# Split weights in whole 2048-column slots, low products last, and a third K-tile pair by sums in each FFN input group

## The chip, the cores and the metric

One core of a Trainium2 chip runs the whole program. The metric is the device time of one execution in microseconds (us); times of a kernel are given as the median of its runs, and the profile is one execution taken by the hardware profiler.

## The reference

256 rows of 2048 features go through one layer of four residual blocks, each followed by a layer norm (`alpha` is 2 to the 1/4):

```
def swiglu_ffn(x, w_in, w_out):
    g, u = jnp.split(x @ w_in, 2, axis=-1)
    return (jax.nn.silu(g) * u) @ w_out
...
h = layer_norm(ALPHA * h + 0.5 * swiglu_ffn(h, ffn1_w_in, ffn1_w_out), ...)
h = layer_norm(ALPHA * h + hybrid_mixer(h, w_in, ...), ...)
h = layer_norm(ALPHA * h + memory_cross_attention(h, mem, ...), ...)
h = layer_norm(ALPHA * h + 0.5 * swiglu_ffn(h, ffn2_w_in, ffn2_w_out), ...)
```

`w_in` of an FFN is 2048 x 11008 (a gate half and an up half of 5504 columns), `w_out` 5504 x 2048. The mixer is two attentions (A: 16 heads of 64 with a bias by distance; B: 16 heads with low-rank queries and keys) whose results are gated and projected; the cross attention has four heads of 512 over 256 memory rows. Everything is float32, and nearly all of the work is products with weight matrices that are read once from HBM.

## The kernel before, in words

**Number format.** A float32 operand is kept as two `float32r` tensors: hi is the rounded value, lo is the remainder. A product of weights W and activations X is made of three matmuls into one PSUM bank: W_hi X_hi, W_lo X_hi and W_hi X_lo. Activations are split when they are made (`Act` holds hi and lo of a K-tile of 128 features side by side). Weights are split as they stream through.

**Streaming.** A weight load is 1 MB, 128 partitions by 2048 columns, into one of three `raw` buffers by SP's queue (line 175). `load` (line 192) splits it in pieces of 1024 columns: ScalarE copies the piece to hi (line 212), VectorE subtracts to make lo (line 215). The pieces lie in four hi slots and four lo slots (`UNITS`, the pools `whi` and `wlo`). `run` walks a list of items, each a function with its weights, and emits loads ahead of use as far as the slots reach. The Tile framework then orders each engine's instructions by their priority and adds semaphores, so the order of an engine comes from the place of an item in the list, from `prio` and from the scheduler.

**FFN input groups.** The 5504 hidden columns are cut into ten groups of 512 and one of 384, and worked in two halves (24 and 19 K-tiles): a half's input groups first, then its output products. An input group has 16 K-tiles, loaded as eight pairs (1 MB: gate and up columns of two K-tiles), and four PSUM banks `ps[tt, g]` (two row halves by up and gate). `mm_pair` issues 24 matmuls of 512 columns per pair, the three products of each bank together (line 296). In ten of the eleven groups of each FFN, the pairs named by `SUMS_IN` go through a scheme with seven block products instead of eight (Strassen's, in Winograd's form): `form_sums` makes a tile of sums of the pair's weights on VectorE (line 183), `mm_sums` (line 340) issues 7 x 3 = 21 matmuls, with forms of the activations made once per FFN (`sum_forms`, lines 307 and 311). Four of the seven results go to the other four PSUM banks, `qs[0]` to `qs[3]`, which all pairs by sums of the group share; after the last one `shared` (lines 602 to 607) turns them into four corrections. `product` (lines 648 to 651) adds these to the four banks and computes silu(gate) x up; `turn` (line 663) transposes the result by TensorE during the next group. Two groups in a row use the two sets of four banks in turn. The weights of a pair by sums and its sums take two slots and the blocks X2 and X3.

**FFN output groups** use the same `pair_group` with their own pairs by sums (`SUMS_OUT`); their forms are made by `forms_step` while the last input groups of the half run.

**Wide products.** Most of the mixer and cross projections use `mm_wide`: stationary W, 16 K-tiles of one 1 MB block, each with a matmul of 512 columns (W_hi by X hi and lo side by side, line 264) and one of 256 columns (W_lo by X_hi, line 265), in turn. The blocks are w_lat 9, w_qk 16, w_gate 32, w_o_b 16, w_xk 16 and w_xq 16 of 16 K-tiles, and w_o_a 16 of eight. `mm_feat` (256 columns, line 253) and `mm_tok` (512 columns, line 284) serve the other products.

**Layer norms** sit between the blocks: VectorE adds the last output columns to the residual, gathers statistics (BN_STATS, BN_AGGR, lines 364 and 369), takes the reciprocal root (lines 348 to 353), scales (line 383, with ScalarE's line 385), and TensorE transposes the rows (line 391) for the next block. Leftover products of the block before fill TensorE during that chain.

## Time and profile before

| | |
|---|---|
| median of 3 runs | 2551.24 us (2547.13 to 2551.26) |
| the profiled execution | 2550.92 us |
| its span, first to last instruction | 2549.2 us |
| mean granted TensorE clock | 0.998 |
| HBM read | 482.69 MB, 190 GB/s over the span |
| DMA queue of the weights, share of 16 engines | 50.5% |

The program is one long stream of weight blocks. A busy share on the page is of the whole span; to see what hides what, one looks at a stretch (a table by windows) or at the rows of an engine in time order (a timeline). A row of the timeline gives the start, the duration, engine, line, operation, output and inputs, how many instructions it stands for, and in brackets how long the engine was idle before it and what released it. The durations of matmuls overlap, since TensorE is a pipeline; what a matmul costs is read from one start to the next. The same holds, less strongly, for queued operations of VectorE.

### The profile page before, as it was taken

What the parts mean: (1) busy time and instruction counts of PE and PEld (TensorE: products, weight loads), DVE (VectorE), ACT (ScalarE), POOL (GpSimd) and SP (SyncE); (2) the same over time, 40 slices, a digit from 0 to 9 for tenths busy, and PEclk for the clock granted to TensorE, in tenths of its full rate; (3) what the DMA queues carried; (4) which work ended last, traced back from release to release, by engine and by line L of the source; (5) the groups of instructions that cost most, each with busy time, mean ns of one, the idle gap of its engine ahead of it and who ended that gap; (6) DMA issues with size and microseconds to landing.
All of it is one profiled execution on the core that took longest, in us unless ns stands there. A gap on an engine that the chain in (4) does not pass through costs nothing.

```text
span 2549.2 us, 32108 instructions
## 1 busy us (share of the span) xinstructions
PE 2533.5 (99%) x12608; PEld 2134.7 (84%) x12608; DVE 1844.1 (72%) x2501; ACT 1279.0 (50%) x1732; POOL 30.0 (1%) x87
## 2 busy tenths in 40 slices
PE   9999999999999999999999999999999999999998
PEld 7888888888888888888888888888888888888886
DVE  6787767788776766555557785555788877787886
ACT  5555445555444555544444564454555554455542
POOL 0000000000000000000000000000000000000000
PEclk9999999999999999999999999999999999999999
DMA  6645554545755643345556565544554555455563
GB/s 252 242 179 207 201 197 172 216 163 217 255 171 177 194 138 116 141 175 189 193 188 256 183 216 196 195 155 146 204 193 181 205 208 198 182 198 198 198 234 130
DMA packets 74184, 488.04 MB, mean 191 GB/s; under 512 B 8625, under 2 KB 8881, under 8 KB 20785
## 3 DMA queue, kind: packets, MB, share of 16 engines
q1 hardware_dynamic: 68496, 467.13, 50.5%
q0 software_dynamic: 3808, 15.73, 2.0%
q10 hardware_dynamic: 1728, 3.15, 0.3%
q8 instruction: 98, 1.61, 0.3%
q14 instruction: 54, 0.43, 0.0%
HBM read 482.69 MB, written 2.10 MB: 190 GB/s over the span
## 4 chain that ended last, share of the span: by engine, by line
PE 97%; DVE 1%; DMA 1%; ACT 0%; issue 0%; ACTq 0%; DVEq 0%; SPq 0%
PE at L296 20%; PE mm L284 19%; PE mm L296 17%; PE mm L264 17%; PE mm L265 8%; PE mm L340 5%; PE at L340 5%; PE mm L253 2%; PE at L865 1%; PE at L748 1%; PE at L895 1%; DMA raw<-ffn_w_in_r 1%; DMA H<-xT 0%; PE at L1165 0%; PE at L1143 0%; PE at L391 0%
## 5 line engine op out<-in xcount | busy, mean ns | idle before, releaser
L215 DVE TENSOR_TENSOR lo<-raw,hi 128x1024 fp32r<-128x1024 f32 (+1 forms) x744 | 896.9, 1213 | 558.7 <-ACT hi L212 548.3
L212 ACT CAST hi<-raw 128x1024 fp32r<-128x1024 f32 (+1 forms) x744 | 773.0, 1044 | 864.2 <-PE at L296 188.4
L264 PE MATMUL mm<-T,hi 128*128 128x512 f32 x1168 | 415.1, 399 | 0.0
L296 PE MATMUL mm<-hi,T 128*128 128x512 f32 (+1 forms) x1088 | 330.1, 380 | 1.0 <-ACT hi L243 1.0
L265 PE MATMUL mm<-T,lo 128*128 128x256 f32 x1168 | 328.2, 281 | 0.0
L296 PE MATMUL at<-hi,T 128*128 128x512 f32 x960 | 300.6, 389 | 0.0
L264 PEld LDWEIGHTS mm<-T,hi 128*128 128x128 f32 x1168 | 219.4, 188 | 55.2 <-issue 1.5
L296 PEld LDWEIGHTS mm<-hi,T 128*128 128x128 f32 x1088 | 202.8, 188 | 36.1 <-ACT hi L243 1.5
L264 PE MATMUL mm<-H,hi 128*128 128x512 f32 x640 | 225.9, 397 | 0.0
L265 PEld LDWEIGHTS mm<-T,lo 128*128 128x128 f32 x1168 | 220.7, 189 | 0.1
L296 PEld LDWEIGHTS at<-hi,T 128*128 128x128 f32 x960 | 180.2, 188 | 37.2
L296 PE MATMUL mm<-lo,T 128*128 128x512 f32 (+1 forms) x544 | 207.5, 381 | 0.4 <-DVE lo L244 0.4
L296 PE MATMUL at<-lo,T 128*128 128x512 f32 x480 | 187.6, 391 | 0.0
L265 PE MATMUL mm<-H,lo 128*128 128x256 f32 x640 | 178.9, 280 | 0.0
L284 PE MATMUL mm<-hi,H 128*128 128x512 f32 x568 | 176.3, 389 | 0.0
L296 PE MATMUL at<-hi,H 128*128 128x512 f32 x560 | 174.8, 389 | 0.0
L264 PEld LDWEIGHTS mm<-H,hi 128*128 128x128 f32 x640 | 120.2, 188 | 29.1
L243 ACT CAST X<-raw 128x1024 fp32r<-128x1024 f32 (+1 forms) x104 | 107.3, 1033 | 71.3 <-DVE raw L183 70.7
L243 ACT CAST hi<-raw 128x1024 fp32r<-128x1024 f32 (+2 forms) x122 | 102.0, 843 | 63.5 <-PE mm L296 29.2
L284 PE MATMUL mm<-hi,X 128*128 128x512 f32 x416 | 130.3, 391 | 0.0
L284 PEld LDWEIGHTS mm<-hi,H 128*128 128x128 f32 x568 | 106.6, 188 | 22.0
L244 DVE TENSOR_TENSOR X<-raw,X 128x1024 fp32r<-128x1024 f32 (+1 forms) x104 | 124.5, 1199 | 0.0
(246 smaller groups left out, 3808.1 us busy)
## 6 DMA issues: line engine op xcount, KB each, us to landing
raw<-ffn_w_in SPq DMA_DIRECT2D x150, 1024.0 KB, 4.6
raw<-ffn_w_out SPq DMA_DIRECT2D x66, 1024.0 KB, 5.2
raw<-w_gate SPq DMA_DIRECT2D x32, 1024.0 KB, 4.8
raw<-ffn_w_out_r SPq DMA_DIRECT2D x16, 1024.0 KB, 4.8
raw<-w_qk SPq DMA_DIRECT2D x16, 1024.0 KB, 4.8
raw<-w_o_b SPq DMA_DIRECT2D x16, 1024.0 KB, 4.7
raw<-w_out SPq DMA_DIRECT2D x16, 1024.0 KB, 4.8
raw<-w_xk SPq DMA_DIRECT2D x16, 1024.0 KB, 4.8
```

The costliest lines, as they stand in the source:

```text
L212: self.nc.scalar.copy(hi[:, :m], raw[:, c:c + m])
L215: self.nc.vector.tensor_tensor(lo[:, :m], raw[:, c:c + m], hi[:, :m].bitcast(F32), ALU.subtract)
L243: self.nc.scalar.copy(hi, src)
L244: self.nc.vector.tensor_tensor(lo, src, hi.bitcast(F32), ALU.subtract)
L253: self.nc.tensor.matmul(ps, w[u][wi][:, c:c + P], x.at(xi, kt), start=(j == 0 and k == 0), stop=(j == n - 1 and k == 2),)
L264: self.nc.tensor.matmul(ps, hi, x.both(kt), start=(kt == 0), stop=False)
L265: self.last_mm = self.nc.tensor.matmul(ps[:, :S], lo, x.at(0, kt), start=False, stop=(kt == n - 1))
L284: self.last_mm = self.nc.tensor.matmul(ps, x.at(xi, kt)[:, tt * P:(tt + 1) * P], w[u][wi][:, c:c + 512], start=(start and j == 0 and k == ...
L296: self.last_mm = self.nc.tensor.matmul(ps[tt, g][:, :n], x.at(xi, kt)[:, tt * P:(tt + 1) * P], hi_lo[wi][:, g * n:(g + 1) * n], start=(kt ...
L340: self.last_mm = self.nc.tensor.matmul(bank[:, :m], a[xi], hi_lo[wi][:, c:c + m], start=own and first and j == 0, stop=own and last and j ...
L748: self.nc.tensor.transpose(ps[:, i * P:(i + 1) * P], s[:, c:c + P], self.ident)
L865: nc.tensor.matmul(ps[:, c0:c0 + nk], q[:, tt * P:(tt + 1) * P], k[:, :nk], start=(j == 0), stop=(j == len(parts) - 1))
```

## The change

1. `UNITS` is 2 and a slot holds 2048 columns. `halves` splits a whole load: ScalarE still copies pieces of 1024, and VectorE makes the lo of the whole load in one subtract (line 236 of the changed kernel: 2048 columns; 1536 for the three raw quarters of a pair by sums, which were pieces of 1024 and 512). Over the program VectorE's subtracts and adds of 1024 columns go from 958 to 106, with 409 new ones of 2048 and 86 of 1536; ScalarE's copies of 1024 go from 902 to 942.
2. In every product all matmuls with W_hi of a block come first and those with W_lo last (`mm_feat`, `mm_wide`, `mm_tok`, `mm_pair`, `mm_sums`).
3. `SUMS_IN` is (2, 4, 6) instead of (2, 5). The forms of the third pair lie in four small work tiles, since the block X0 holds two. The three adds of the weights are one of 1024 and two of 512 as before, formed one load ahead; the sums are split into X2 (hi) and X3 (lo) of 2048 columns. Of the program's matmuls, 12424 become 12364.
4. `held` counts slots of the new size. The weights `w_nope` of attention B come two heads to a 1 MB load, which stays in its slot for the odd head; SP's loads go from 476 to 467.

The same in the code:

```diff
-SUMS_IN = (2, 5)
+SUMS_IN = (2, 4, 6)
...
-UNITS = 4
+UNITS = 2
...
         def slots(w):
-            if isinstance(w, Sums):
-                return 2
-            return 0 if w[1] else -(-w[0].shape[1] // 1024)
+            return 0 if isinstance(w, tuple) and w[1] else 1
...
         def form_sums(i):
-            raw, t, m = fetch(i), self.raw_tile(), queue[i].m
-            for a, b, c in ((slice(0, 2 * m), raw[:, 0:2 * m], raw[:, m:3 * m]),
-                            (slice(2 * m, 3 * m), t[:, 0:m], raw[:, 2 * m:3 * m]),
-                            (slice(3 * m, 4 * m), t[:, 2 * m:3 * m], raw[:, 3 * m:4 * m])):
-                self.nc.vector.tensor_tensor(t[:, a], b, c, ALU.add)
-            sums[i] = []
-            for k in range(2):
-                blk = self.block(SUM_TAGS[k], (P, 2, 1024), F32R)
-                self.split(t[:, k * 2 * m:(k + 1) * 2 * m], blk[:, 0, :2 * m], blk[:, 1, :2 * m])
-                sums[i].append((blk[:, 0, :], blk[:, 1, :]))
+            if i < len(queue) and isinstance(queue[i], Sums) and i not in sums:
+                raw, t, m = fetch(i), self.raw_tile(), queue[i].m
+                two = [v.rearrange("p (a m) -> p a m", a=2) for v in (t[:, :2 * m], raw[:, m:3 * m])]
+                self.nc.vector.tensor_tensor(two[0], two[1], raw[:, :m].unsqueeze(1).to_broadcast([P, 2, m]), ALU.add)
+                for a, b in ((2, 0), (3, 2)):
+                    self.nc.vector.tensor_tensor(t[:, a * m:a * m + m], t[:, b * m:b * m + m],
+                                                 raw[:, a * m:a * m + m], ALU.add)
+                sums[i] = t
         def load(i):
             w = queue[i]
             raw = fetch(i)
-            for k in (i, i + 1):
-                if k < len(queue) and isinstance(queue[k], Sums) and k not in sums:
-                    form_sums(k)
-            got = []
+            form_sums(i)
             if isinstance(w, Sums):
-                for a, b in ((2 * w.m, 4 * w.m), (0, w.m)):
-                    hi, lo = self.unit()
-                    self.split(raw[:, a:b], hi[:, :b - a], lo[:, :b - a])
-                    got.append((hi, lo))
-                return got + sums[i]
-            ap, tags = w
-            n = ap.shape[1]
-            if tags:
-                blk = [self.block(g, (P, 2048), F32R) for g in tags[:2]]
-            step = 768 if ap.tensor.name.endswith("_w_in_r") else 1024
-            for c in range(0, n, step):
-                m = min(step, n - c)
-                hi, lo = [x[:, c:c + step] for x in blk] if tags else self.unit()
-                self.nc.scalar.copy(hi[:, :m], raw[:, c:c + m])
-                with self.tc.issue_after(self.chain.ins) if self.chain is not None else nullcontext():
-                    self.nc.vector.tensor_tensor(lo[:, :m], raw[:, c:c + m], hi[:, :m].bitcast(F32), ALU.subtract)
-                got.append((hi, lo))
+                n = 4 * w.m
+                got = self.halves(raw[:, w.m:n], *self.unit()), self.halves(
+                    sums[i][:, :n], *(self.block(g, (P, 2048), F32R) for g in SUM_TAGS))
+            else:
+                ap, tags = w
+                hi, lo = (self.block(g, (P, 2048), F32R) for g in tags[:2]) if tags else self.unit()
+                got = self.halves(raw[:, :ap.shape[1]], hi, lo)
+            form_sums(i + 1)
...
-            units = [u for _ in ws for u in ready.pop(0)]
+            got = [ready.pop(0) for _ in ws]
             live -= sum(slots(queue[done + i]) for i in range(len(ws)))
             done = need
...
+    def halves(self, src, hi, lo):
+        n = src.shape[1]
+        for c in range(0, n, 1024):
+            d = min(c + 1024, n)
+            self.nc.scalar.copy(hi[:, c:d], src[:, c:d])
+        with self.tc.issue_after(self.chain.ins) if self.chain is not None else nullcontext():
+            self.nc.vector.tensor_tensor(lo[:, :n], src, hi[:, :n].bitcast(F32), ALU.subtract)
+        return hi, lo
...
     def mm_wide(self, ps, w, x, n=KT):
+        hi, lo = ([v[:, kt * P:(kt + 1) * P] for kt in range(n)] for v in w)
         for kt in range(n):
-            c = kt % 8 * P
-            hi, lo = (u[:, c:c + P] for u in w[kt // 8])
-            self.nc.tensor.matmul(ps, hi, x.both(kt), start=(kt == 0), stop=False)
-            self.last_mm = self.nc.tensor.matmul(ps[:, :S], lo, x.at(0, kt), start=False, stop=(kt == n - 1))
+            self.nc.tensor.matmul(ps, hi[kt], x.both(kt), start=(kt == 0), stop=False)
+        for kt in range(n):
+            self.last_mm = self.nc.tensor.matmul(ps[:, :S], lo[kt], x.at(0, kt), start=False, stop=(kt == n - 1))
...
     def mm_pair(self, ps, w, n, x, kts, nk=KT):
-        for (hi_lo, kt) in zip(w, kts):
-            for tt in range(2):
-                for g in range(2):
-                    for k, (wi, xi) in enumerate(((0, 0), (1, 0), (0, 1))):
-                        self.last_mm = self.nc.tensor.matmul(
-                            ps[tt, g][:, :n], x.at(xi, kt)[:, tt * P:(tt + 1) * P],
-                            hi_lo[wi][:, g * n:(g + 1) * n],
-                            start=(kt == 0 and k == 0), stop=(kt == nk - 1 and k == 2),
-                        )
+        for wi in range(2):
+            for j, kt in enumerate(kts):
+                for tt in range(2):
+                    for g in range(2):
+                        c = (2 * j + g) * n
+                        for xi in range(2 - wi):
+                            self.last_mm = self.nc.tensor.matmul(
+                                ps[tt, g][:, :n], x.at(xi, kt)[:, tt * P:(tt + 1) * P], w[wi][:, c:c + n],
+                                start=(kt + wi + xi == 0), stop=(kt == nk - 1 and wi == 1),
+                            )
...
-        self.split(f, out[:, 0], out[:, 1])
+        if isinstance(out, list):
+            for j in range(4):
+                self.split(f[:, j], out[j][:, 0], out[j][:, 1])
+        else:
+            self.split(f, out[:, 0], out[:, 1])
...
-                e["f"] = self.block(tag, (P, len(at), 2, 4, P), F32R)
-            self.sum_forms(x(), 2 * at[i], e["f"][:, i])
+                e["block"] = self.block(tag, (P, 2, 2, 4, P), F32R)
+            out = e["block"][:, i] if i < 2 else [self.w1((P, 2, P), F32R) for _ in range(4)]
+            self.sum_forms(x(), 2 * at[i], out)
+            e[i] = [[out[:, a, j, :] if i < 2 else out[j][:, a] for a in (0, 1)] for j in range(4)]
...
-        n5, s2, n3, s3 = ([forms[:, a, j, :] for a in (0, 1)] for j in range(4))
-        for bank, a, (hi_lo, c), own in (
-                (ps[0, 0], plain(k + 1, 0), (u1, m), False),
-                (ps[0, 1], n3, (u1, 0), False),
-                (qs[0], plain(k, 0), (u2, 0), True),
-                (qs[1], n5, (t13, 0), True),
-                (qs[3], s3, (t13, m), True),
-                (qs[2], s2, (t24, 0), True),
-                (ps[1, 0], plain(k + 1, 1), (t24, m), False)):
-            for j, (wi, xi) in enumerate(((0, 0), (1, 0), (0, 1))):
-                self.last_mm = self.nc.tensor.matmul(
-                    bank[:, :m], a[xi], hi_lo[wi][:, c:c + m],
-                    start=own and first and j == 0, stop=own and last and j == 2)
+        n5, s2, n3, s3 = forms
+        for v, parts in (
+                (w[0], ((ps[0, 0], plain(k + 1, 0), 2, False),
+                        (ps[0, 1], n3, 1, False),
+                        (qs[0], plain(k, 0), 0, True))),
+                (w[1], ((qs[1], n5, 0, True),
+                        (qs[3], s3, 1, True),
+                        (qs[2], s2, 2, True),
+                        (ps[1, 0], plain(k + 1, 1), 3, False)))):
+            for wi in range(2):
+                for bank, a, c, own in parts:
+                    for xi in range(2 - wi):
+                        self.last_mm = self.nc.tensor.matmul(
+                            bank[:, :m], a[xi], v[wi][:, c * m:(c + 1) * m],
+                            start=own and first and wi + xi == 0, stop=own and last and wi == 1)
...
-        held = [2 * sum(g is None for g in tags[:j]) for j in range(5)]
+        held = [sum(g is None for g in tags[:j]) for j in range(5)]
...
-            def fn(w):
+            def fn(w=None):
+                if h % 2 == 0:
+                    kept[h + 1] = w
+                else:
+                    w = kept.pop(h)
                 for k in range(2):
                     ps = self.mm_tile()
-                    self.mm_feat(ps[:, :S], w, [(0, k * 512 + j * P) for j in range(4)], self.c,
-                                 range(4 * k, 4 * k + 4))
+                    c = h % 2 * 1024 + k * 512
+                    self.mm_feat(ps[:, :S], w, [c + j * P for j in range(4)], self.c, range(4 * k, 4 * k + 4))
                     v = self.w1()
                     (nc.scalar.copy if k == 0 else nc.vector.tensor_copy)(v, ps[:, :S])
                     bq[h, k] = v
-            self.add(fn, t["w_nope"][h])
-        def b_scores(h):
+            self.add(fn, *(() if h % 2 else (t["w_nope"][h // 2],)), held=h % 2)
+        def b_scores(h, held):
...```

The order of instructions shows it at three places. First VectorE at the end of an input group of the first FFN (`w` are the work tiles of `shared`, `mm` the banks of `qs`, X the low half of the sums, `lo` the low half of a load). Before:

```order
L244 TENSOR_TENSOR lo_1314<-raw_1265,hi_1313 128x512
L215 TENSOR_TENSOR lo_1344<-raw_1341,hi_1343 128x1024
L215 TENSOR_TENSOR lo_1348<-raw_1341,hi_1347 128x1024
L215 TENSOR_TENSOR lo_1375<-raw_1372,hi_1374 128x1024
L604 TENSOR_TENSOR w_244_1384<-w_242_1382,mm_1240 128x512
L215 TENSOR_TENSOR lo_1379<-raw_1372,hi_1378 128x1024
L605 TENSOR_TENSOR w_243_1383<-w_243_1383,w_244_1384 128x512
```

And in the changed kernel:

```order
L236 TENSOR_TENSOR X_189_1293<-raw_1262,X_188_1292 128x2048
L236 TENSOR_TENSOR lo_1324<-raw_1321,hi_1323 128x2048
L603 TENSOR_TENSOR w_198_1358<-w_196_1356,mm_1196 128x512
L236 TENSOR_TENSOR lo_1352<-raw_1349,hi_1351 128x2048
L604 TENSOR_TENSOR w_197_1357<-w_197_1357,w_198_1358 128x512
L605 TENSOR_TENSOR w_198_1358<-w_198_1358,mm_1197 128x512
```

The combinations (604 to 607 before, 603 to 606 now) followed the low half of pair 6 and a part of pair 7's; now they follow pair 7's, and a subtract of 2048 columns, the low half of the next group's first pair, stands inside them where one of 1024 stood.

Second, VectorE where an output group's forms are made during an input group (`L307` and `L311` before, `L300` and `L304` now; X is the low half of the sums of weights, or of the forms where it is 512 wide). Before:

```order
L244 TENSOR_TENSOR X_190_1121<-raw_1117,X_190_1121 128x1024
L651 SCALAR_TENSOR_TENSOR w_181_1048<-w_180_1047,w_181_1048 128x512
L244 TENSOR_TENSOR X_191_1124<-raw_1117,X_191_1124 128x1024
L215 TENSOR_TENSOR lo_1128<-raw_1113,hi_1127 128x1024
L215 TENSOR_TENSOR lo_1132<-raw_1113,hi_1131 128x1024
L311 TENSOR_TENSOR w_198_1137<-w_197_1136 128x128 x2
L311 TENSOR_TENSOR w_198_1137<-w_198_1137,w_197_1136 128x128
```

And in the changed kernel:

```order
L182 TENSOR_TENSOR raw_1082<-raw_1082,raw_1080 128x512
L304 TENSOR_TENSOR w_156_1088<-w_155_1087 128x128
L182 TENSOR_TENSOR raw_1082<-raw_1082,raw_1080 128x512
L304 TENSOR_TENSOR w_156_1088<-w_156_1088,w_155_1087 128x128
L304 TENSOR_TENSOR w_156_1088<-w_155_1087 128x128
L304 TENSOR_TENSOR w_156_1088<-w_155_1087,w_156_1088 128x128
L236 TENSOR_TENSOR lo_1133<-raw_1080,hi_1132 128x1536
L226 TENSOR_TENSOR X_154_1086<-w_156_1088,X_154_1086 128x512
L236 TENSOR_TENSOR X_164_1138<-raw_1082,X_163_1137 128x2048
```

The forms came after the low halves of the sums and now come before them.

Third, TensorE at the start of the mixer, where `mm_wide` begins (`T` are the normed activations, `hi` and `lo` the block's halves). Before:

```order
L264 MATMUL mm_5846<-T_971_5397,hi_5769 128x512
L265 MATMUL mm_5846<-T_971_5397,lo_5770 128x256
L264 MATMUL mm_5846<-T_971_5397,hi_5769 128x512
L265 MATMUL mm_5846<-T_971_5397,lo_5770 128x256
L264 MATMUL mm_5846<-T_971_5397,hi_5769 128x512
```

And in the changed kernel:

```order
L256 MATMUL mm_5496<-T_749_5066,hi_5425 128x512 x4
L256 MATMUL mm_5496<-T_750_5067,hi_5425 128x512 x4
L256 MATMUL mm_5496<-T_751_5068,hi_5425 128x512 x4
L256 MATMUL mm_5496<-T_752_5069,hi_5425 128x512 x4
L258 MATMUL mm_5496<-T_749_5066,lo_5426 128x256 x4
```

The two widths took turns and now stand in two series, sixteen of 512 columns and then sixteen of 256.

82 lines of the change are left out of this document (41 added, 41 removed).

## The prediction

> **What bounds the kernel now.** First the page: the busy share of each engine, the granted clock by slices, and the chain that ended last.
>
> ```profile
> span 2549.2 us, 32108 instructions
> ...
> PE 2533.5 (99%) x12608; PEld 2134.7 (84%) x12608; DVE 1844.1 (72%) x2501; ACT 1279.0 (50%) x1732; POOL 30.0 (1%) x87
> ...
> PEclk9999999999999999999999999999999999999999
> ...
> PE 97%; DVE 1%; DMA 1%; ACT 0%; issue 0%; ACTq 0%; DVEq 0%; SPq 0%
> ```
>
> TensorE is busy for 99% of the span, holds 97% of the chain, and its clock is full in every slice. So time leaves this kernel only if TensorE gets less to do, and comes in only where TensorE is made to wait. The second view is a table by windows: two input groups in a row of the first FFN, and the two stretches of the mixer that matter here.
>
> ```profile
> core 0: us, PE busy (x) PEld busy (x) DVE busy (x) ACT busy (x) POOL busy (x), PEclk, DMA share, GB/s
> 143.99:187.16 43.17, 43.17 (x195) 35.63 (x194) 36.09 (x44) 23.28 (x27) 0.00 (x0) 1.00 0.51 195
> 187.16:230.33 43.17, 43.17 (x195) 35.64 (x194) 34.59 (x39) 22.74 (x26) 0.00 (x0) 1.00 0.52 195
> 925.00:1054.00 129.00, 128.79 (x791) 105.16 (x790) 84.11 (x205) 66.45 (x165) 2.01 (x9) 1.00 0.34 117
> 1054.00:1400.00 346.00, 346.00 (x1923) 298.87 (x1922) 211.42 (x292) 165.46 (x238) 2.12 (x4) 1.00 0.55 199
> ```
>
> A steady input group lasts 43.17 us with no gap on TensorE, while VectorE is busy for 34.6 to 36.1 us, 80 to 84%. That is the cover of the first edit, and it is the smallest in the program. In the mixer (1054 to 1400) VectorE has 61%.
>
> Third, the timeline of TensorE, for the step from one matmul to the next: 512 columns in series, 256 in series, then the two in turn as `mm_wide` issues them.
>
> ```profile
> 663.03 0.39 PE L284 MATMUL mm<-lo,H 128*128 128x512 f32 x1
> 663.26 0.62 PE L284 MATMUL mm<-hi,H 128*128 128x512 f32 x2
> ...
> 667.79 0.39 PE L284 MATMUL mm<-lo,H 128*128 128x512 f32 x1
> ```
> ```profile
> 980.72 0.28 PE L253 MATMUL mm<-X,lo 128*128 128x256 f32 x1
> 980.84 0.40 PE L253 MATMUL mm<-X,hi 128*128 128x256 f32 x2
> ...
> 983.23 0.28 PE L253 MATMUL mm<-X,lo 128*128 128x256 f32 x1
> ```
> ```profile
> 1315.09 0.40 PE L264 MATMUL mm<-T,hi 128*128 128x512 f32 x1
> 1315.32 0.28 PE L265 MATMUL mm<-T,lo 128*128 128x256 f32 x1
> 1315.44 0.40 PE L264 MATMUL mm<-T,hi 128*128 128x512 f32 x1
> ...
> 1317.21 0.40 PE L264 MATMUL mm<-T,hi 128*128 128x512 f32 x1
> ```
>
> The pattern of one and two repeats seven times between the first and the last row of the first fence: 21 matmuls in 4.76 us, 0.2267 us each. The second: 21 in 2.51 us, 0.1195 each. The third: six pairs in 2.12 us, 0.353 a pair, which is 0.007 more than 0.2267 + 0.1195 = 0.3462. Inside a pair the 512 takes about 0.235 and the 256 about 0.117.
>
> **Part 1, the third pair by sums.** Of each input group's eight pairs, three instead of two go from 24 to 21 matmuls. There are 18 groups of 512 columns and two last groups of 384: 18 x 3 x 0.2267 = 12.2 us, and 2 x 3 x 0.173 = 1.0 (the 384 step, between the two series by columns, an estimate from them). Together -13.3 us. The adds are on VectorE and have to be hidden there. Its prices:
>
> ```profile
> L215 DVE TENSOR_TENSOR lo<-raw,hi 128x1024 fp32r<-128x1024 f32 x718 | 873.3, 1223 | 540.2 <-ACT hi L212 530.1
> ...
> L183 DVE TENSOR_TENSOR raw<-raw,raw 128x512 f32<-128x512 f32 x96 | 66.0, 688 | 1.4
> ...
> L183 DVE TENSOR_TENSOR raw<-raw 128x1024 f32<-128x1024 f32 x48 | 58.7, 1222 | 2.7 <-DMA raw<-ffn_w_in 2.0
> ```
> ```profile
> 212.69 0.69 DVE L604 TENSOR_TENSOR w<-w,at 128x512 f32<-128x512 f32 x1 [0.48 <-PE at L340]
> 213.29 1.22 DVE L215 TENSOR_TENSOR lo<-raw,hi 128x1024 fp32r<-128x1024 f32 x1
> 214.43 0.68 DVE L605 TENSOR_TENSOR w<-w,w 128x512 f32<-128x512 f32 x1
> ```
>
> Queued one behind the other, an operation of 512 columns steps by 213.29 - 212.69 = 0.60 us and one of 1024 by 214.43 - 213.29 = 1.14. No row of 2048 or 1536 columns exists before. By the slope between the two rows 2048 costs 1.14 + 2 x 0.54 = 2.21 and 1536 costs 1.67; from above, two separate operations of 1024 are 2.45 by their durations. I take 2.20, since the slope is measured on the same operation. The Trainium skill, "VectorE: DVE Perf Modes", section "Side-by-side: where the cycles go for N=2048 bf16", gives about 2293 ns for a 2048-column operation in the regular mode; by it eight of them would add 0.7 us to a group's work on VectorE, and no run here shows that length yet.
>
> VectorE per group afterwards: five plain pairs at 2.20 = 11.0; three by sums at 1.14 + 2 x 0.60 (adds) + 1.67 + 2.20 (subtracts) = 6.2, 18.6 together; the `shared` combinations 4 x 0.60; `product` 6 x 0.60; the turned low halves 2 x 0.60. Sum 36.8. The same sum for before gives 33.5 where the window shows 34.6, so I add 1.1: 37.9 us, 89% of a group that now takes 43.17 - 0.68 = 42.5. It still fits, so the gain should arrive nearly whole.
>
> The tightest place is the low half X3 of the first pair by sums. Behind the end of the last pair of the group before, VectorE does `product` (3.6 and about 0.7 of waiting for ScalarE's activation), the low half of pair 1 (2.2), the adds (2.3), the subtracts of 1536 (1.7) and 2048 (2.2), with about 1 us in which ScalarE copies the second half of X2: 13.7. TensorE meanwhile has pairs 0 and 1 (2 x 24 x 0.2267 = 10.9), eight transposes (0.9) and 17 products of pair 2 (3.9): 15.7. There is room of 2.0. In four of the 22 input groups VectorE's order now puts the forms of the next output group (one 512, four 128, one 512 low half) ahead of that X3:
>
> ```profile
> L311 DVE TENSOR_TENSOR w<-w,w 128x128 f32<-128x128 f32 x24 | 6.8, 284 | 0.0
> ...
> L311 DVE TENSOR_TENSOR w<-w 128x128 f32<-128x128 f32 x24 | 6.0, 285 | 0.1
> ...
> L307 DVE TENSOR_TENSOR w<-H 128x512 f32<-128x512 f32 x8 | 5.5, 686 | 0.0
> ```
>
> That is 2.1 to 2.5 us, and so a stall of 0 to 1.5 us each. TensorE's order has some products of the next pair ahead of the last X3 products there, so I take 0.4: +1.5 over four.
>
> **Part 2, low products last in `mm_wide`.** 105 weight blocks of 16 K-tiles and 16 of eight. A block of 16 takes 16 x 0.353 = 5.65 us now; in series 15 x (0.2267 + 0.1195) and one change-over of 0.353 make 5.55. That is -0.097 x 105 = -10.2, and -0.05 x 16 = -0.8; with the medians of the whole trace (0.352) it is 1.3 less. I take -10. From below: were only the 256 to keep its price of 0.1195 and the 512 its 0.235, it would cost 121 blocks about +3. In `mm_pair`, `mm_tok` and `mm_feat` all products of a block have one width, and their order changes nothing: 0.
>
> **Part 3, whole slots.** Two slots of 2048 instead of four of 1024: capacity is the same. A plain pair's hi slot comes free after 16 of 24 matmuls, 3.6 us into 5.4; its next user starts 5.4 us after the pair's end, 7.3 us later, and ScalarE's copies and the subtract take 2.0 + 2.2. In `mm_wide` 3.6 of 5.55, the same. The raw buffers are still three, and a group uses them 11 times in place of ten (eight loads, three sums), 42.5 x 3 / 11 = 11.6 us for each use; a load holds one for its landing, two copies and one subtract:
>
> ```profile
> raw<-ffn_w_in SPq DMA_DIRECT2D x150, 1024.0 KB, 4.6
> raw<-ffn_w_out SPq DMA_DIRECT2D x66, 1024.0 KB, 5.2
> ```
>
> 4.6 + 2.0 + 2.2 = 8.8, at 5.2 it is 9.4, and some 2 more where sums are formed: 0. The two-head loads of `w_nope` (a mixer stretch of 129.0 us with 128.79 busy) halve the issues on SP's queue and move no matmul: 0, at most 0.5 either way.
>
> **Part 4, the layer-norm joints.** TensorE there goes to the transposes as soon as the scaled rows are out:
>
> ```profile
> 697.67 1.00 DVE L383 TENSOR_SCALAR h<-h,mv,y 128x512 f32<-128x512 f32 x2
> 697.79 1.52 ACT L385 ACTIVATE h<-h,nb,y 128x512 f32<-128x512 f32 x2 [5.93 <-DVE nb L373]
> 698.62 1.02 PEld L391 LDWEIGHTS at<-ident,h 128*128 128x128 f32 x8
> 698.85 1.03 PE L391 MATMUL at<-ident,h 128*128 128x128 f32 x8
> ```
>
> The weights for the transposes load the moment VectorE's 1.00 us ends (698.67), so there is at most 0.2 us of room. At two of the joints a 2.2 us subtract now stands inside the statistics chain, where 1.1 us pieces were just outside it: 0 to 2 us each, +1.5 together.
>
> Sum against the profiled execution: 2550.9 - 13.3 - 10 + 1.5 + 1.5 = **2531 us**. The profiled execution lies 0.3 below the median of the runs, so it serves for that too. No change could not be told from what lies within 0.2%, 5 us.
>
> **Rivals.** *A: the order in `mm_wide` brings nothing.* If a pair's 0.353 belongs to the two widths and not to their turns, the -10 goes: 2541. Against it stand the three measured steps; for it, that 7 ns a pair is little, and that the 256 steps are read from another line with other weights. 0.13. [...]
>
> *B, the slower side: VectorE's order sets the pace of the input groups.* Before, VectorE is idle 8.6 of 43.17 us in a group, in waits such as these:
>
> ```profile
> 191.98 1.23 DVE L215 TENSOR_TENSOR lo<-raw,hi 128x1024 fp32r<-128x1024 f32 x1 [1.76 <-ACT hi L212]
> ...
> 206.95 1.23 DVE L215 TENSOR_TENSOR lo<-raw,hi 128x1024 fp32r<-128x1024 f32 x1 [2.27 <-ACT hi L212]
> 209.68 2.54 DVE L215 TENSOR_TENSOR lo<-raw,hi 128x1024 fp32r<-128x1024 f32 x2 [1.50 <-ACT hi L212]
> ```
>
> Afterwards there is room for 42.5 - 37.9 = 4.6 us of waits. If they shrink only to 6.5, because each waits for a slot that TensorE frees and not for VectorE's own lateness, a group is 1.9 us longer: 20 x 1.9 = +38 on 2531, or 2569. It decides from 4.6 us of waits a group, and makes the kernel slower than before from about 5.7. Against it: these waits come from VectorE running ahead, and vanish when it is late. 0.07.
>
> *C: the banks of the third pair.* The sums' results lie in the other four PSUM banks until `shared` has taken them. The last pair by sums was pair 5, with two pairs (10.9 us) behind it before the next group writes these banks; now it is pair 6 with one (5.4). VectorE's chain there is 0.6, a subtract of 2.2 that its order puts between, and 3 x 0.6: 4.6 and ScalarE's copy of 0.6. By my count it just fits, because the first six products of the next group need only banks that are free earlier. Late by 1 us in each of 20 groups: 2551. 0.08.
>
> **How the numbers follow.** Forecast 0.72, A 0.13, C 0.08, B 0.07. The forecast's own range is 2525 (no stall and the dearer change-over) to 2538; A reaches 2545 with stalls. These two hold 0.85, so the range is 2525 to 2546. Faster by more than 5 us (below 2546): forecast and A, 0.85, and 0.01 of C. Within 5 us: most of C, 0.07. Slower: B, 0.07.
>
> **What would show it.** Right: the window of a steady group is 42.4 to 42.6 us with TensorE busy throughout and VectorE at 37 to 39; the `mm_wide` lines step by 0.227 and 0.1195, so the stretch from 1054 to 1400 is 2 us or so shorter for each 20 blocks; subtracts of 2048 step by 2.2. Wrong: idle time on TensorE ahead of the L340 products released by X3 (B), or ahead of the seventh matmul of a group released by line 606 (C); a 512 step of 0.235 in series, or a 256 step above 0.12 (A); more than 2 us lost at a joint.

## The result, and the profile after

The changed kernel takes 2530.52 us (median of 6 runs, 2528.53 to 2531.95) where the kernel before takes 2550.55 (6 runs, 2546.39 to 2551.26): a ratio of 0.9924, 95% interval 0.9912 to 0.9936. The forecast was 2531 in a range of 2525 to 2546. Runs of the kernel before lie in two groups on every chip, near 2547 and from 2550.5 to 2554, for a reason that is open; against the lower group the change is worth some 16 us, against the upper some 20 to 21. So below, a difference of a few us is read from the traces or from variants of the changed kernel.

First the page of the changed kernel: span, busy shares, and the chain that ended last.

```profile
span 2530.1 us, 31424 instructions
...
PE 2511.6 (99%) x12548; PEld 2126.5 (84%) x12548; DVE 1873.7 (74%) x2118; ACT 1288.9 (51%) x1780; POOL 29.8 (1%) x87
...
PE 95%; DMA 2%; DVE 2%; ACT 0%; issue 0%; DVEq 0%; ACTq 0%; SPq 0%
```

TensorE still holds the chain, with 60 matmuls less; VectorE has 30 us more work in 383 fewer instructions. Added up from each start to the next, TensorE's steps go from 2535.5 to 2516.5 us. Then the windows of three input groups, from the first transpose of one to that of the next.

```profile
core 0: us, PE busy (x) PEld busy (x) DVE busy (x) ACT busy (x) POOL busy (x), PEclk, DMA share, GB/s
147.38:189.81 42.43, 42.43 (x192) 35.17 (x191) 38.23 (x34) 23.45 (x29) 0.00 (x0) 1.00 0.55 201
189.81:232.22 42.41, 42.41 (x193) 35.18 (x192) 37.70 (x33) 23.98 (x29) 0.00 (x0) 1.00 0.54 200
...
1924.45:1966.85 42.40, 42.40 (x192) 35.18 (x191) 38.59 (x38) 23.72 (x29) 0.00 (x0) 1.00 0.51 193
```

A group is 42.4 us where it was 43.17, without a gap, and VectorE has 37.7 to 38.6 us of it (37.4 to 38.8 over all groups of 512 columns in which TensorE does not wait). The timeline of VectorE inside the second of these groups shows the new prices.

```profile
200.26 2.29 DVE L236 TENSOR_TENSOR X<-raw,X 128x2048 fp32r<-128x2048 f32 x1 [0.98 <-ACT X L233]
202.47 2.29 DVE L236 TENSOR_TENSOR lo<-raw,hi 128x2048 fp32r<-128x2048 f32 x1
204.68 1.22 DVE L180 TENSOR_TENSOR raw<-raw 128x1024 f32<-128x1024 f32 x1
...
206.54 1.75 DVE L236 TENSOR_TENSOR lo<-raw,hi 128x1536 fp32r<-128x1536 f32 x1
208.21 0.69 DVE L182 TENSOR_TENSOR raw<-raw,raw 128x512 f32<-128x512 f32 x1
...
220.06 0.68 DVE L606 TENSOR_TENSOR w<-w,at 128x512 f32<-128x512 f32 x1
```

A subtract of 2048 columns steps by 204.68 - 202.47 = 2.21 and lasts 2.29; one of 1536 steps by 1.67. The bracket on X shows the wait for ScalarE's second copy, about 1 us.

The timeline of TensorE in the same group, around the pair by sums 4 and at the next group's start, and in the mixer where `mm_wide` runs:

```profile
202.97 1.52 PE L340 MATMUL at<-X,X 128*128 128x512 f32 x6
204.33 0.61 PE L340 MATMUL mm<-X,T 128*128 128x512 f32 x2
204.78 0.84 PE L340 MATMUL at<-X,X 128*128 128x512 f32 x3
```
```profile
219.52 1.98 PE L290 MATMUL mm<-lo,T 128*128 128x512 f32 x8
221.33 3.79 PE L290 MATMUL at<-hi,T 128*128 128x512 f32 x16
```
```profile
1307.88 3.82 PE L256 MATMUL mm<-H,hi 128*128 128x512 f32 x16
1311.53 2.08 PE L258 MATMUL mm<-H,lo 128*128 128x256 f32 x16
1313.44 3.82 PE L256 MATMUL mm<-T,hi 128*128 128x512 f32 x16
```

The ninth product with X (the first with the low half X3) starts at 204.78, and X3 was ready at 200.26 + 2.29 = 202.55: 2.2 us of room. The last combination, line 606, ends at 220.74, before the next group begins at 221.33. A block of `mm_wide` is 1313.44 - 1307.88 = 5.56 us: 3.65 for sixteen of 512 columns and 1.91 for sixteen of 256.

What TensorE waited for in the whole trace, summed by line (us in total, times, longest us):

```profile
PE mm L290 <- ACT hi L225: 1.6, 2, 0.9
PE mm L340 <- DVE H L226: 1.2, 1, 1.2
PE at L391 <- DVE h L383: 1.1, 2, 0.9
...
PE at L290 <- ACT hi L233: 0.7, 1, 0.7
```

The row of line 391 is the layer-norm joints. The row of line 340 is a wait in the second FFN that no step of the prediction names (below).

### The profile page after: what moved, and what is told of

It reads as the page before. It is cut to its first block, busy times and chain, and to the rows that moved or that the text cites. A ratio compares the mean times of both kernels' runs of the same rounds, so it can differ in the third digit from the quotient of the medians.

```text
span 2530.1 us, 31424 instructions
## 1 busy us (share of the span) xinstructions
PE 2511.6 (99%) x12548; PEld 2126.5 (84%) x12548; DVE 1873.7 (74%) x2118; ACT 1288.9 (51%) x1780; POOL 29.8 (1%) x87
## 4 chain that ended last, share of the span: by engine, by line
PE 95%; DMA 2%; DVE 2%; ACT 0%; issue 0%; DVEq 0%; ACTq 0%; SPq 0%
PE at L290 18%; PE mm L256 16%; PE mm L277 16%; PE mm L290 16%; PE mm L258 9%; PE mm L340 7%; PE at L340 6%; PE mm L246 2%; PE at L864 1%; DVE lo L236 1%; PE at L747 1%; PE at L894 1%; DMA H<-xT 0%; PE at L1171 0%; PE at L1149 0%; PE at L391 0%
## 5 line engine op out<-in xcount | busy, mean ns | idle before, releaser
L236 DVE TENSOR_TENSOR lo<-raw,hi 128x2048 fp32r<-128x2048 f32 (+3 forms) x433 | 924.9, 2136 | 438.0 <-ACT hi L233 426.9
L233 ACT CAST hi<-raw 128x1024 fp32r<-128x1024 f32 (+1 forms) x848 | 813.6, 1004 | 746.1 <-PE mm L277 165.7
L256 PE MATMUL mm<-T,hi 128*128 128x512 f32 x1168 | 280.6, 392 | 0.0
L256 PEld LDWEIGHTS mm<-T,hi 128*128 128x128 f32 x1168 | 214.7, 188 | 43.6 <-issue 1.5
L233 ACT CAST X<-raw 128x1024 fp32r<-128x1024 f32 (+1 forms) x156 | 157.6, 1029 | 175.2 <-DVE raw L182 86.3
L290 PE MATMUL mm<-hi,T 128*128 128x512 f32 (+1 forms) x928 | 214.2, 380 | 1.6 <-ACT hi L225 1.6
L236 DVE TENSOR_TENSOR X<-raw,X 128x2048 fp32r<-128x2048 f32 (+1 forms) x78 | 174.3, 2236 | 54.4 <-ACT X L233 53.2
L290 PEld LDWEIGHTS mm<-hi,T 128*128 128x128 f32 x928 | 172.0, 188 | 32.5 <-ACT hi L225 2.2
L290 PE MATMUL at<-hi,T 128*128 128x512 f32 x800 | 192.7, 389 | 0.0
L290 PEld LDWEIGHTS at<-hi,T 128*128 128x128 f32 x800 | 150.1, 188 | 31.3
L258 PEld LDWEIGHTS mm<-T,lo 128*128 128x128 f32 x1168 | 150.0, 191 | 5.7
L256 PE MATMUL mm<-H,hi 128*128 128x512 f32 x640 | 154.5, 391 | 0.0
L258 PE MATMUL mm<-T,lo 128*128 128x256 f32 x1168 | 152.1, 283 | 0.0
L256 PEld LDWEIGHTS mm<-H,hi 128*128 128x128 f32 x640 | 117.1, 188 | 22.4
L290 PE MATMUL at<-hi,H 128*128 128x512 f32 x560 | 133.2, 390 | 0.7 <-ACT hi L233 0.7
L290 PEld LDWEIGHTS at<-hi,H 128*128 128x128 f32 x560 | 104.9, 188 | 22.7 <-ACT hi L233 1.0
L290 PE MATMUL mm<-lo,T 128*128 128x512 f32 (+1 forms) x464 | 110.4, 380 | 0.0
L290 PE MATMUL at<-lo,T 128*128 128x512 f32 x400 | 99.0, 389 | 0.0
L182 DVE TENSOR_TENSOR raw<-raw,raw 128x512 f32<-128x512 f32 (+1 forms) x144 | 97.5, 677 | 1.7
```

The lines of the kernel that those rows point to most:

```text
L182: self.nc.vector.tensor_tensor(t[:, a * m:a * m + m], t[:, b * m:b * m + m], raw[:, a * m:a * m + m], ALU.add)
L233: self.nc.scalar.copy(hi[:, c:d], src[:, c:d])
L236: self.nc.vector.tensor_tensor(lo[:, :n], src, hi[:, :n].bitcast(F32), ALU.subtract)
L256: self.nc.tensor.matmul(ps, hi[kt], x.both(kt), start=(kt == 0), stop=False)
L258: self.last_mm = self.nc.tensor.matmul(ps[:, :S], lo[kt], x.at(0, kt), start=False, stop=(kt == n - 1))
L290: self.last_mm = self.nc.tensor.matmul(ps[tt, g][:, :n], x.at(xi, kt)[:, tt * P:(tt + 1) * P], w[wi][:, c:c + n], start=(kt + wi + xi == 0 ...
```

## The experiments

By their chip numbers the first four ran on one chip, the three with more work for VectorE and the one on `w_nope` on a second, the pieces and the earlier transposes on a third, and the last two, the changed kernel itself among them, on the second number again. Each is the changed kernel with one edit, unless it says otherwise. A difference of medians across chips is rougher than one between traces, so both are given where they part. Sums over lines of TensorE are made from each start to the next.

### Two pairs by sums again

```diff
-SUMS_IN = (2, 4, 6)
+SUMS_IN = (2, 5)
```

> The changed kernel with two pairs by sums (2, 5) instead of three. If the terms add up on TensorE alone, 60 matmuls come back: 18 x 3 x 0.2267 + 2 x 3 x 0.173 = +13.3 us on 2530.5, 2543.8 (2541 to 2546). If the third pair's gain was partly eaten by VectorE or the PSUM banks, less comes back: 2536 to 2540. If the whole slots were worth something by themselves, it stays under 2541 too, but then the input groups of this kernel are as long as those of before, 43.1 to 43.2 us.

2543.97 us (2542.99 to 2546.01, 11 runs), ratio to the kernel before 0.9974 (0.9965 to 0.9983). Its steady groups:

```profile
191.80:235.00 43.20, 43.20 (x196) 35.66 (x194) 34.01 (x28) 22.16 (x27) 0.00 (x0) 1.00 0.54 195
235.00:278.08 43.08, 43.08 (x195) 35.70 (x194) 33.56 (x33) 22.22 (x28) 0.00 (x0) 1.00 0.53 190
```

The groups are as long as those of before, so slots and order give nothing in there; the third pair gives the 0.7 us. In the trace TensorE's steps add up to 11.1 us more than in the changed kernel, not 13.3: by the lists of waits the changed kernel has 2.2 us more of them, net.

### The two widths of mm_wide in turn again

```diff
         for kt in range(n):
             self.nc.tensor.matmul(ps, hi[kt], x.both(kt), start=(kt == 0), stop=False)
-        for kt in range(n):
             self.last_mm = self.nc.tensor.matmul(ps[:, :S], lo[kt], x.at(0, kt), start=False, stop=(kt == n - 1))
```

> The changed kernel with the two widths of mm_wide in turn again. If the order is worth what the steps say, the 121 blocks lose 7 to 10 us: 2537.5 to 2540.5, and a pair steps by 0.352 to 0.354 again. If the order is worth nothing and the gain of these lines came from elsewhere: 2529.5 to 2531.5.

2571.02 us (2567.38 to 2574.62, 5 runs), ratio 1.0085 (1.0070 to 1.0099): 40 us slower than the changed kernel (35.5 by TensorE's steps), and slower than the kernel before. Neither expectation held. Its timeline at the start of a block, its mixer by windows, and as long a stretch of the mixer in the changed kernel:

```profile
1102.67 0.50 PE L256 MATMUL mm<-T,hi 128*128 128x512 f32 x1 [0.84 <-ACT hi L233]
...
1103.45 0.38 PE L257 MATMUL mm<-H,lo 128*128 128x256 f32 x1 [0.27 <-DVE lo L236]
```
```profile
1060.00:1400.00 340.00, 321.65 (x1777) 273.55 (x1778) 186.74 (x225) 149.78 (x221) 2.12 (x4) 0.99 0.52 187
```
```profile
1050.00:1390.00 340.00, 340.00 (x1914) 298.55 (x1913) 205.24 (x239) 164.11 (x240) 2.11 (x4) 1.00 0.57 201
```

TensorE waits at the start of a block for the hi copies and then, one matmul later, for the low half: 18 us of idle in 340. With the widths in turn both halves are needed at once and both slots come free only at the block's end; in series the hi slot is free after 3.65 of 5.56 us, and the low half is needed 3.65 us later. With two whole slots the order is not worth 10 us but 40, and the waits are what it saves: behind the wait for the low half the pairs of this run do not step by 0.352 to 0.354.

```profile
1109.69 0.40 PE L256 MATMUL mm<-T,hi 128*128 128x512 f32 x1
...
1117.31 0.40 PE L256 MATMUL mm<-T,hi 128*128 128x512 f32 x1
```

Between these two rows lie 22 pairs in turn, 0.346 us each, no dearer than the two steps in series.

### The order alone, in the kernel before

```diff
+        hi, lo = ([w[kt // 8][i][:, kt % 8 * P:kt % 8 * P + P] for kt in range(n)] for i in range(2))
         for kt in range(n):
-            c = kt % 8 * P
-            hi, lo = (u[:, c:c + P] for u in w[kt // 8])
-            self.nc.tensor.matmul(ps, hi, x.both(kt), start=(kt == 0), stop=False)
-            self.last_mm = self.nc.tensor.matmul(ps[:, :S], lo, x.at(0, kt), start=False, stop=(kt == n - 1))
+            self.nc.tensor.matmul(ps, hi[kt], x.both(kt), start=(kt == 0), stop=False)
+        for kt in range(n):
+            self.last_mm = self.nc.tensor.matmul(ps[:, :S], lo[kt], x.at(0, kt), start=False, stop=(kt == n - 1))
```

> The kernel before with mm_wide in series and nothing else. If the order alone is worth what the steps say: 2550.6 - 7 to 10 = 2540.5 to 2543.5. If it needs the whole slots (TensorE waits, since four slots of 1024 come free in another order): 2545 to 2551. If the order is worth nothing: 2549.5 to 2551.5.

2542.91 us (2542.47 to 2543.97, 9 runs), ratio 0.9974 (0.9964 to 0.9983): 4 to 9 us faster than the kernel before. Its blocks:

```profile
1314.96 3.82 PE L263 MATMUL mm<-H,hi 128*128 128x512 f32 x16
1318.61 2.08 PE L265 MATMUL mm<-H,lo 128*128 128x256 f32 x16
1320.52 3.82 PE L263 MATMUL mm<-T,hi 128*128 128x512 f32 x16
```

Again 5.56 us a block. The order gives its gain with four slots of 1024 too; over all 121 blocks the two lines lose 7.9 us (639.2 to 631.3), and TensorE's steps in all 7.7. So rival A, that the order brings nothing, is settled.

The price of the turn is not a property of the two widths, though. In the trace of the kernel before, an uninterrupted run of pairs in turn keeps to one of two paces from its beginning to its end: 0.353 us a pair, or 0.347 (288 of the 1808 pairs, 224 of them in fourteen of the sixteen blocks of `w_xk`). One block of `w_xk` in the kernel before, from its first matmul to that of the next block:

```profile
1507.96 0.39 PE L264 MATMUL mm<-H,hi 128*128 128x512 f32 x1
...
1513.50 0.39 PE L264 MATMUL mm<-H,hi 128*128 128x512 f32 x1
```

That is 5.54 us for sixteen pairs in turn, no more than the 5.56 in series. The sixteen blocks of `w_xk` took 89.3 us in turn and take 89.4 in series. In the kernel before, the runs that begin behind the small transposes (line 391) or behind line 815 (the sums of squares of a norm) have the lower pace, and those behind `mm_tok` and all other lines the higher; in the run with the widths in turn again one of the four behind the transposes has the higher too, so what decides it is open. The order gains only where the higher pace was.

### The low products inside the block again

The inner loops of `mm_pair`, `mm_tok`, `mm_feat` and `mm_sums` issue the three products of a bank together; `mm_wide` stays in series. For `mm_pair`:

```diff
-        for wi in range(2):
-            for j, kt in enumerate(kts):
-                for tt in range(2):
-                    for g in range(2):
-                        c = (2 * j + g) * n
-                        for xi in range(2 - wi):
...
+        for j, kt in enumerate(kts):
+            for tt in range(2):
+                for g in range(2):
+                    c = (2 * j + g) * n
+                    for k, (wi, xi) in enumerate(((0, 0), (1, 0), (0, 1))):
...
```

> The changed kernel with the three products of each bank together again in mm_pair, mm_tok, mm_feat and mm_sums, so that the hi slot comes free at a block's end and not after two thirds of it; mm_wide stays in series. If only widths count on TensorE and the slots have room: 2529.5 to 2531.5, no idle time. If it is low-last that gives two whole slots their room: copies and subtract, 2.0 + 2.2, plus what is queued, no longer fit into the 5.4 us of one pair, and each input group loses 1 us or more: 2545 to 2575, with TensorE waiting for the low half of a plain pair.

2541.68 us (2540.55 to 2543.57, 8 runs), ratio 0.9972 (0.9961 to 0.9983): 11 us slower than the changed kernel by the medians and 7.8 by TensorE's steps, between the two expectations. What TensorE waited for first of all:

```profile
PE mm L275 <- DVE lo L236: 3.5, 4, 1.3
PE mm L287 <- DVE lo L236: 1.4, 2, 0.7
```

Steady groups are hardly longer (42.44 and 42.71 us). The waits are for low halves, most in `mm_tok` (line 275), whose lines are 4.6 us longer; those of the pairs are 4.1 longer. The kernel before, with the same order and four slots, has no such wait in `mm_tok`. So in these products, whose matmuls are all of one width, the order is what lets two whole slots do the work of four.

### More work for VectorE: one subtract twice, two twice, a fourth pair

```diff
                 got = self.halves(raw[:, :ap.shape[1]], hi, lo)
+                if self.again(ap):
+                    self.nc.vector.tensor_tensor(lo[:, :ap.shape[1]], raw[:, :ap.shape[1]],
+                                                 hi[:, :ap.shape[1]].bitcast(F32), ALU.subtract)
...
```

`again` picks pair 3 of each full input group, and in the second run pairs 3 and 7.

> The changed kernel with the subtract of pair 3 of each full input group made twice (18 groups, 2.2 us more for VectorE in each: 40.1 of 42.4). If VectorE's 4.7 idle us in a group are room, the time stays at 2530 to 2533. If they are waits that its order fixes (rival B), each group is 2.2 us longer: 2570.

> As the run before, with the subtracts of pairs 3 and 7 both made twice: 42.3 us of work for VectorE in a group of 42.4. If idle time is room, TensorE waits only for what cannot shrink (about 1 us in each pair by sums, ScalarE's second copy): groups of 43.5 to 45.5, 2550 to 2586. If all waits stay: 18 x 4.4 = +79, 2610.

```diff
-SUMS_IN = (2, 4, 6)
+SUMS_IN = (1, 3, 5, 6)
...
+            if i == 3:
+                e[3] = e[2]
+                return
```

> The changed kernel with four pairs by sums, (1, 3, 5, 6); the fourth uses the third's forms, its own being left out for want of space. TensorE has 41.7 us a group, 13.3 us less over the program; VectorE 4.0 more a group, 41.9. If VectorE then sets the pace with its waits of about 1 us in each pair by sums: groups of 43 to 46 and 2540 to 2600, so three is where the scheme ends. If the waits give way: 2517 to 2522.

One subtract twice: 2552.10 us (2550.59 to 2557.77, 12 runs), ratio 1.0014 (1.0005 to 1.0023). Two: 2588.28 (2585.90 to 2589.70, 5 runs), ratio 1.0155 (1.0140 to 1.0170). Four pairs: 2600.14 (2596.24 to 2601.94, 4 runs), ratio 1.0198 (1.0181 to 1.0214). Windows of groups of each, in this order:

```profile
192.81:236.69 43.88, 43.17 (x193) 34.94 (x192) 39.62 (x34) 24.01 (x28) 0.00 (x0) 1.00 0.55 194
236.69:280.46 43.77, 43.06 (x192) 34.87 (x191) 40.05 (x36) 24.87 (x29) 0.00 (x0) 1.00 0.57 197
```
```profile
198.34:243.54 45.20, 43.40 (x192) 34.80 (x191) 41.62 (x35) 23.85 (x29) 0.00 (x0) 1.00 0.54 185
243.54:288.70 45.16, 43.67 (x192) 34.55 (x191) 41.77 (x35) 25.33 (x30) 0.00 (x0) 1.00 0.55 195
```
```profile
132.26:179.57 47.31, 43.64 (x189) 34.06 (x188) 43.66 (x43) 26.18 (x32) 0.00 (x0) 1.00 0.52 179
179.57:226.27 46.70, 43.60 (x189) 33.75 (x188) 41.78 (x37) 25.43 (x31) 0.00 (x0) 1.00 0.52 181
```

The first lies between its two expectations, the second just above the first of its two and well below 2610, and the third at the upper end of its first. Each time TensorE's group grows, and VectorE is still idle for 3.4 to 4.9 us of it. Idle time does shrink when VectorE gets more to do, from 8.6 us in the window that the prediction read to 3.8 to 4.7 in the changed kernel, but in these groups it goes hardly further. In the run with two, VectorE's own waits in its first window are:

```profile
DVE X L245 <- ACT X L242: 2.8, 3, 1.1
DVE lo L245 <- ACT hi L242: 0.7, 1, 0.7
```

Three times it waits for ScalarE's copy of the sums, which cannot start before VectorE has made the sums. By this window VectorE fills a group of 42.4 us with about 42.4 - 3.5 = 38.9 us of work, an estimate, where the groups shown of the changed kernel have 37.7 to 38.6. The run with one subtract twice says about the same: of its 2.2 us more a group, the steady groups shown pay 1.4 to 1.5. It is no fixed limit: the same run has a group of 42.66 us, early in the second FFN, with 40.10 us of VectorE's work and no wait of TensorE.

Nor do these runs measure VectorE's room alone. A subtract made twice also finishes its own result 2.2 us later, and in the run with one TensorE waits most for just that result (line 199 is the repeat; total, times, longest):

```profile
PE at L299 <- DVE lo L199: 5.8, 6, 1.4
```

With four pairs, 5 and 6 follow each other on the one set of blocks X2 and X3, and in the second window above ScalarE's copy of the sums waits 1.7 us for the subtract that still reads X2; the fourth pair's forms are left out, so its products are not the right ones and only the time counts. Against the run of the changed kernel on the same chip number (2532.66 us, below) the three cost 19, 56 and 67 us. So rival B's mechanism, waits that VectorE's own order fixes, is there, and by the estimate the change stops about 1 us of VectorE's work a group short of it; how much of the three costs is a full VectorE, and how much a late result or a shared block, was not separated. A fourth pair placed so costs 67 us where it takes 13 from TensorE.

### The heads of w_nope one to a load, and the low half in pieces

```diff
-            self.add(fn, *(() if h % 2 else (t["w_nope"][h // 2],)), held=h % 2)
+            self.add(fn, t["w_nope"][h // 2, :, h % 2 * 1024:h % 2 * 1024 + 1024])
...
```

> The changed kernel with w_nope again one head to a load of 512 KB. The prediction gave this part 0, at most 0.5 us. The trace shows the lines of attention B (246, 864, 894, 747, 895) 2.7 us shorter in all than before. If the two-head loads did that: 2533, and the lines are back at 131 to 132 us from 129.1; if it came from the order of the products: 2530.5 and 129.

2533.85 us (2531.44 to 2534.64, 5 runs), ratio 0.9938 (0.9924 to 0.9951). The five lines of attention B are at 129.1 us (131.8 before), as in the changed kernel, so the two-head loads did not shorten them; TensorE's steps add up to 0.4 us less than in the changed kernel. The kernel before with the order alone has these lines shorter too, at 129.4 us. The time agrees with the first expectation, but it does not part the two: the changed kernel itself, on the same chip number, gave 2532.66 (below), and the runs overlap.

```diff
             self.nc.scalar.copy(hi[:, c:d], src[:, c:d])
-
-        with self.tc.issue_after(self.chain.ins) if self.chain is not None else nullcontext():
-            self.nc.vector.tensor_tensor(lo[:, :n], src, hi[:, :n].bitcast(F32), ALU.subtract)
+            with self.tc.issue_after(self.chain.ins) if self.chain is not None else nullcontext():
+                self.nc.vector.tensor_tensor(lo[:, c:d], src[:, c:d], hi[:, c:d].bitcast(F32), ALU.subtract)
```

> The changed kernel with the low half subtracted in pieces of 1024 again, each right behind its copy. VectorE has 8 x 0.07 = 0.6 us more a group (2 x 1.14 against 2.21), 38.5 of 42.4. If work alone counts, with 1 to 2 us of margin left: 2530 to 2533. If the wide subtract's wait for ScalarE's second copy (1.1 us in each pair by sums) is what fills VectorE, the pieces start a copy earlier, the waits shrink by more than 0.6, and nothing is lost: 2528.5 to 2531, VectorE idle in a group as before or more. If the number of operations counts more than that: 2535 or above, TensorE waiting for low halves.

2534.08 us (2532.63 to 2534.47, 5 runs), ratio 0.9944 (0.9932 to 0.9957): by the trace 2.6 us more than the changed kernel, between the first expectation and the third. Steady groups mostly stay at 42.4 us, with 38.5 and 40.1 us of VectorE's work in two of them, and the new waits are of one kind:

```profile
PE mm L339 <- DVE H L226: 4.3, 4, 2.0
```

It is the same wait as the unexpected one after the change: for the low half of the transposed result. The wide subtract in place of pieces is worth these 2.6 us, and steady groups do not need it.

### The transposes one pair earlier

The transposes of a group's result lie in a PSUM bank of the other set, and `mm_sums` needs all four of that set as `qs` in the same pair. The bank is free when VectorE has made the low half from it. The trace of the changed kernel where TensorE waits for that, in the second FFN's first group with sums:

```profile
1884.80 0.39 PE L290 MATMUL at<-hi,T 128*128 128x512 f32 x1
1885.63 0.68 DVE L226 TENSOR_TENSOR H<-mm,H 128x512 fp32r<-128x512 f32 x1
...
1886.36 0.96 PE L340 MATMUL mm<-X,X 128*128 128x512 f32 x3 [1.18 <-DVE H L226]
```

```diff
-                self.weave(main, {2: [turn]} if turn else {}, prio=0)
+                self.weave(main, {1: [turn]} if turn else {}, prio=0)
```

> The changed kernel with the transposes of a group's result one pair earlier in the next input group, so that their PSUM bank is free sooner. The trace shows one wait of 1.2 us in the second FFN for that bank. If the bank is the cause, the wait is gone and nothing else waits: 2529 to 2530.5, which the time alone can hardly show. If the transposes come too early for the product (4.4 us of VectorE and ScalarE behind the last pair, 5.4 us of TensorE's work): a wait of up to 1 us in each of 20 groups, 2531 to 2550.

2530.59 us (2528.12 to 2532.80, 5 runs), ratio 0.9933 (0.9920 to 0.9947), at the upper end of the first expectation. No wait for line 226 is left, and TensorE's steps add up to 4.1 us less. To see whether that is real it ran again beside the changed kernel:

> The changed kernel itself, beside the next run on one chip: 2528.5 to 2532.

> The changed kernel with the earlier transposes, beside the changed kernel on one chip. Its trace had 4.1 us less on TensorE (the waits for the transposes' bank, 2.7 us in the lines of the pairs by sums, and 1 us at the end of the last input group). If that is real, it is 2 to 4 us below the run beside it; if the traces differ by chance, within 1 us.

The changed kernel: 2532.66 us (2531.46 to 2532.73, 5 runs), ratio 0.9938 (0.9924 to 0.9953). With earlier transposes: 2530.08 (2527.21 to 2533.57, 5 runs), ratio 0.9930 (0.9916 to 0.9943). What TensorE waited for, the changed kernel first:

```profile
PE mm L340 <- DVE H L226: 2.2, 2, 1.5
PE mm L290 <- ACT hi L225: 1.8, 2, 1.3
...
PE at L391 <- DVE h L383: 1.0, 2, 0.8
PE at L340 <- DVE H L226: 0.5, 1, 0.5
```
```profile
...
PE mm L290 <- ACT hi L225: 0.6, 2, 0.5
...
PE at L391 <- DVE h L383: 0.2, 1, 0.2
```

The bank is the cause of the wait: it is gone both times, and TensorE's steps are 5.7 us shorter in this pair of traces. The medians differ by 2.6 us, but the runs overlap, so by time it is only likely that this version is the faster one; it is below the kernel before by all of its runs.

## Why the prediction was right

**TensorE as the bound, time only through its work.** Right: the steady groups are as much shorter as the matmuls that left them, and the kernel with two pairs again has its old groups back.

**The sum.** Right in the main, and in part lucky in its size. Part 1 came out 2 us and part 2 about 3 us smaller than forecast, and lines of attention B that no term had gave 2.7 us. The 2550.9 us that it starts from belongs to the upper of the two groups of runs of the kernel before.

**Part 1, -13.3.** The count was right. The run with two pairs shows 11.1 us net in the traces (medians 11.3 and 13.4 us apart, from the changed kernel's two sets of runs): 2.2 us go to waits. The forecast had 1.5 for waits, but for another one. X3 of the first pair by sums was priced at 0 to 1.5 us in four groups; no line shows a wait for it. Its room, foreseen as 2.0, is 2.2 at pair 4, and more at pair 2, where TensorE's order defers those products. What did come is the wait for the bank of the transposes, 1.2 us once (2.7 in the second trace), 0.7 us for ScalarE's first copy where the output products begin, and 0.9 us more for ScalarE's hi of the transposed result (line 225). No step named this bank, though rival C spoke of the very same four.

**Part 1, VectorE's prices.** 2048 columns at 2.20 and 1536 at 1.67: measured 2.21 and 1.67. Group work 37.9: measured 37.4 to 38.8. But "it still fits" was argued from 4.6 us of idle time, and that step was weak: most of the idle time left in a group is waits on ScalarE that VectorE's order fixes, 3.5 us in the window worked out above. The sum came out right because the work stayed below the 38.9 us estimated there, by about 1 us in most groups; nothing in the prediction had worked that out.

**Part 2, -10.** The order does save time, but the term was too large: 7.1 us on the two lines (639.2 to 632.1), 7.9 with the order alone. Its own numbers give 0.102 us a block, not the 0.097 written, and so 11.5 in all. Two things are missing from it. The 0.353 a pair was read from six pairs and used for all, but 288 of the 1808 pairs already ran at 0.347, most of them in the blocks of `w_xk`, which gained nothing. And the change-over costs more than one pair: behind a series of 256, the first five steps of 512 in the changed kernel are 0.233, 0.236, 0.228, 0.232 and 0.231 by their medians, and only then 0.227, so a clean block is 5.56 to 5.57 in place of 5.55. Of the 2.7 us in the lines of attention B, the order alone gives 2.4; with the widths in turn again, 1.3 come back. Why the small matmuls there run closer was not settled.

**Part 3, 0.** Right in sum, for a reason that the text put too lightly. It counted that a slot comes free after two thirds of a block, and did not say what the change would cost without that: 11 us (7.8 by the traces) where the low products go back inside the block, and 40 where `mm_wide` goes back in turn. With two whole slots the order of part 2 is a condition of part 3.

**Part 4, +1.5.** 1.1 us at two joints, 0.9 the longest, where the kernel before shows no such wait. That the wide subtract inside the chain makes it, as the step says, is not shown: the wait is 0.3 us with the subtract in pieces, but 0.2 with the earlier transposes, where the wide subtract stands.

**The rivals.** A, that the order brings nothing, fell by the order alone, though in the `w_xk` blocks it does bring nothing. C fell: in the group shown, line 606 ends 0.6 us before the next group begins, and no wait for it is on the list. B did not happen, but is the neighbour: it put the fixed waits at 6.5 us a group where these runs show about 3.5, and one more subtract a group costs 19 us.

## What to carry to other kernels

Idle time of a helper engine is not room. Room is the distance of each of its results from the matmul that needs it, less the waits that its own order fixes. Giving the engine more to do tries it, if one also asks which result that makes late; here a group with some 4.7 us of idle time paid 1.4 to 1.5 us for 2.2 us more work. When buffers become fewer and larger, look at when each half comes free and when it is first needed: an order of products can be what makes the buffers suffice. And read a price over all the rows that it will be used for: six pairs showed one pace of two.

## What the runs showed of the hardware that was not expected

A series of 512-column matmuls behind one of 256 needs five steps to settle (0.233, 0.236, 0.228, 0.232, 0.231, then 0.227 us in the changed kernel), and the first step of a series of 256 behind one of 512 is 0.113 in place of 0.120. In turn the two widths have two paces, 0.353 and 0.347 us a pair, the second as cheap as the settled steps, 0.227 + 0.120. A run of pairs kept its pace until something stood between, in the kernel before once for 1768 matmuls, and in the run with the widths in turn again the pairs behind a wait for the low half had the cheaper one. What sets the pace was not tried.
